# A two-layer transformer block on one core: weights times v in one row per attention unit, and the LayerNorm scale and shift between the layers applied when the rows are read back

## The chip, the cores and the metric

The kernel runs on one NeuronCore of a Trainium2 chip. The metric is device time in microseconds of one execution: 1528.76 us, the median of 3 runs (1528.45 to 1531.19). The engines are written as the profile writes them: PE (TensorE's products, PEld its weight loads), DVE (VectorE), ACT (ScalarE), POOL (GpSimd) and SP (SyncE, which issues the DMAs).

## The reference, cut to what matters

256 latent tokens and 256 context tokens of width 1024 go through two layers. In layer 1 only the latent tokens are carried on past the attention.

```python
for l in range(DEPTH):                       # DEPTH = 2
    o = token_mixer(x * (1 + sc1) + sh1, ...)   # A: windowed attention, B: global attention, C: RG-LRU,
                                                # three gated branches, one output projection
    x = layernorm(ALPHA * x + g1 * o, ln1_g[l], ln1_b[l])
    x = layernorm(ALPHA * x + g2 * mlp(x * (1 + sc2) + sh2), ln2_g[l], ln2_b[l])

def layernorm(x, g, b): return (x - mean) * rsqrt(var + eps) * g + b
def attend(q, k, v):    p = exp(s - m); return (p @ v) / sum(p)     # s = q @ k / 8, plus mask and sink in A
```

Everything is computed in float32. The attention has 8 query heads and 2 key heads in A and in B; one key head serves 4 query heads.

## The kernel before, in words

**Products.** A float32 operand is split into a high and a low part (`whi`, `wlo` for weights, `h_hi`, `h_lo` for rows), and each product is three passes: high by high, high by low, low by high. `mm` (L92) issues them, `tp` (L99) the transposes. The split is a cast (L120 on ACT or L122 on DVE) and a subtraction on DVE (L128). Projections with output channels on the partitions write a PSUM bank `ps_cm`, those with tokens on the partitions `ps_tm`. Weights arrive as units of 1 MB or less in the buffers `raw` (three of them, DMA at L186), are split piece by piece while the unit ahead of them is multiplied, and PE takes them in a fixed order.

**Attention.** The work of branches A and B is cut into units `(branch, key head, block of 128 tokens)`: 16 in layer 0 (8 of latent, 8 of context tokens) and 8 in layer 1. A unit has steps: its four heads of q transposed (`q_stage`, `ps_qT`); two score steps (`s_step`, `ps_s`, with the softmax on DVE and ACT after them); for each block of 128 keys (4 for a latent unit, 2 for a context unit) a transposing step (`t_step`: four transposes into `ps_pT`, then one copy on ACT into a tile `pT`); and a step of weights times v (`pv_step`: two products of 128 rows by 64 columns into the two halves of `ps_pv`). These two products are the ones that are not split in parts: they are plain float32, and PE shows two records for each. After a unit's last one the result is split into `y_hl`.

**The order of the work.** `attention` yields one step at a time, and `pair` interleaves it with projection work (the q projections of B, then the gates and branches of `MERGE[l]`). A step becomes due by a clock `self.pe` that adds a planned cost for each product: weights times v of one key block `lag_t` (3500 in layer 0, 2500 in layer 1) after that block's transposes, each transposing step at least `pace_t` (700) after the last one. So the key blocks of a unit are multiplied with v one at a time, with projection work, transposes or scores between them:

```python
if un["pv"] < un["t"]:
    opts.append((un["t_at"][un["pv"]] + lag_t, "pv"))
```

A scheduler then orders each engine's instructions under their dependencies; the buffers come from pools that rotate (63 tiles of 128x512 in the pool `gen`).

**LayerNorm between the layers.** After layer 0's MLP, `ln_z` (L1219, DVE) makes the normalised rows without scale and shift; the next layer's projections take scale and shift with their own modulation. The rows themselves are needed again 350 us later, as the residual of layer 1's output projection, with the scale and shift in them. `ln_x(0, 2)` does this at the start of layer 1, in the RG-LRU part (`lru`): it loads four tiles of scale and shift rows (`ln_rows`, L412), multiplies and adds on POOL (L1261, L1262, 8 instructions of 128x512), and writes the rows to DRAM (`xd`, L1263). `wout(1)` reads them back (L1334) at the start of the output projection. In that RG-LRU part PE needs the split weights of the first units, and DVE does the short convolution (L638), the splits of its result (`xc_hi`, `xc_lo`) and part of the weight splits.

Of the kernel before, what the change touches and what calls it, by code (L numbers as in the profile page):

```python
# [11 lines left out]
ALU = mybir.AluOpType  # L12
# [35 lines left out]
class Kern:  # L48
# [987 lines left out]
    def attention(self, l):  # L1036

        todo = deque((br, gr, tb) for br in "AB" for gr in range(2) for tb in ((2, 3, 0, 1) if l == 0 else (2, 3)))  # L1040
        left = {br: sum(u[0] == br for u in todo) for br in "AB"}
        live = []
        s_next = t_next = 0.0
        lag_q, lag_s, lag_t, pace_s, pace_t, depth_u = self.LAGS[l]
        while todo or live:
            now, soonest, step = self.pe, None, None
            for un in live:
                u, st = un["u"], un["st"]
                opts = []
                if un["pv"] < un["t"]:  # L1050
                    opts.append((un["t_at"][un["pv"]] + lag_t, "pv"))
                if un["s"] == 2 and un["t"] < un["n"]:
                    opts.append((max(un["s_at"] + lag_s, t_next), "t"))
                if un["s"] < 2:
                    opts.append((max(un["q_at"] + lag_q, s_next), "s"))
                for at, what in opts:
                    if at <= now:
                        step = (un, what)
                        break
                    soonest = at if soonest is None else min(soonest, at)  # L1060
                if step:
                    break
            if step is None and todo and len(live) < depth_u:
                u = todo[0]
                br, gr, tb = u
                ready = (l, "k", br) in self.flags and (l, "q") + u in self.flags
                if ready and now < self.qs_at[u] + (0, 4000)[l] and not self.idle_filler:
                    yield "wait"
                    continue
                if ready:  # L1070
                    if tb == 2:
                        self.k_stage(br, gr)
                        if gr == 0:
                            self.y[br] = [self.g2(l, "y_hl", F32R) for _ in range(4)]
                    todo.popleft()
                    self.q_stage(u)
                    live.append(dict(u=u, st=dict(p=[], pt={}, kt=self.kt), s=0, t=0, pv=0, n=4 if tb >= 2 else 2,
                                     t_at=[], q_at=self.pe))
                    yield
                    continue  # L1080
                if not live:
                    yield "need"
                    continue
            if step is None:
                if self.idle_filler:

                    self.pe = soonest
                else:
                    yield "wait"
                continue  # L1090
            un, what = step
            u, st = un["u"], un["st"]
            if what == "pv":
                last = un["pv"] == un["n"] - 1
                self.pv_step(u, un["pv"], st, last)
                un["pv"] += 1
                if last:
                    live.remove(un)
                    left[u[0]] -= 1
                    if left[u[0]] == 0:  # L1100
                        self.flags.add((l, "y", u[0]))
            elif what == "t":
                self.t_step(u, un["t"], st)
                un["t"] += 1
                un["t_at"].append(self.pe)
                t_next = self.pe + pace_t
            else:
                self.s_step(u, 2 * un["s"], st)
                un["s"] += 1
                un["s_at"] = self.pe  # L1110
                s_next = self.pe + (pace_s if u[2] >= 2 else pace_s / 2)
                if un["s"] == 2:
                    self.qt.pop(u)
            yield
# [134 lines left out]
    def ln_x(self, l, which):  # L1249


        nc = self.nc
        g, b = self.ln_rows(l, which)
        for tb in (range(4) if which == 1 and l == 0 else range(2, 4)):
            for hf in range(2):
                z = self.x[tb][hf]
                if which == 1:
                    for row, op in ((g[hf], ALU.mult), (b[hf], ALU.add)):
                        self.bg.append((2000, lambda z=z, row=row, op=op: nc.gpsimd.tensor_tensor(z, z, row, op=op), False))
                    continue  # L1260
                nc.gpsimd.tensor_tensor(z, z, g[hf], op=ALU.mult)  # L1261
                nc.gpsimd.tensor_tensor(z, z, b[hf], op=ALU.add)  # L1262
                nc.sync.dma_start(out=self.xd[128 * (tb - 2):128 * (tb - 1), 512 * hf:512 * hf + 512], in_=z)  # L1263

    def tail_units(self, l, which, keys, xs):

# [57 lines left out]

    def wout(self, l):
        self.start_residual(l, 1)
        self.x = {}
        for tb in self.tbs:
            r = slice(128 * (tb % 2), 128 * (tb % 2) + 128)
            src = (self.a["ctx"][0], self.a["x"][0])[tb // 2] if l == 0 else self.xd  # L1330
            self.x[tb] = []
            for hf in range(2):
                t = self.g("x")
                self.nc.sync.dma_start(out=t, in_=src[r, 512 * hf:512 * hf + 512])  # L1334
                self.x[tb].append(t)
        for h in range(2):
            self.unit((l, "wo", 0, h), self.take((l, "wo", 0, h)), self.m_hl(), self.tbs, True)
        self.tail_units(l, 1, [(l, "wo", 1, 0), (l, "wo", 1, 1)], self.m_hl())
        self.m = {}
# [110 lines left out]
    def layer(self, l):  # L1450
        a = self.a
        self.ada_start("layer%d" % l)
        self.layer_consts(l)
        self.ks, self.qs, self.qt, self.vv, self.y, self.m, self.tg, self.qs_at = {}, {}, {}, {}, {}, {}, {}, {}
        self.lru(l)
        if l == 0:
            self.run(self.kv(l, "A"))
            self.run(self.q(l, "A", 0))
            self.run(self.kv(l, "B"))

        def filler():
            if l == 0:
                yield from self.q(l, "A", 1)
            yield from self.q(l, "B", 0)
            yield from self.q(l, "B", 1)
            brs = [br for what, br in self.MERGE[l] if what == "br"]
            for what, br in self.MERGE[l]:
                self.ada_start(what + br + str(l))
                if what == "g":
                    yield from self.merge_gates(l, br)  # L1470
                else:
                    yield from self.merge_branch(l, br, br == brs[0], br == brs[-1])

        fl = filler()
        self.pair(self.attention(l), fl, (1.2, 2.0)[l])
        for _ in fl:
            pass
        self.h = None
        self.wout(l)
        self.ada_start("mlp%d" % l)  # L1480
        self.mlp(l)
# [95 lines left out]
```

## Time and profile before

| | |
|---|---|
| median of 3 runs | 1528.76 us |
| the profiled execution, its own time | 1529.95 us |
| span of that execution | 1528.2 us |
| PE busy | 1475.7 us, 97% |
| DVE busy | 1189.1 us, 78% |
| ACT busy | 743.7 us, 49% |
| POOL busy | 292.4 us, 19% |
| granted PE clock, mean | 0.985 |

One execution is profiled, and all durations below come from it; its own time is 1.75 us over its span. Columns of a timeline row are start (us from the span's start), duration (us), engine, line, operation, the tile written and those read, shapes, count, and in brackets how long the engine stood idle before it and what released it. Records of PE overlap, since the products are pipelined: what one costs is read from the distance of the starts. A row with `x4` stands for four records in a row. In rows by form, the number after `x` is the count, then busy us and the mean ns of one.

### The profile page before, as it was taken

What the parts mean: (1) busy time and instruction counts of PE and PEld (TensorE: products, weight loads), DVE (VectorE), ACT (ScalarE), POOL (GpSimd) and SP (SyncE); (2) the same over time, 40 slices, a digit from 0 to 9 for tenths busy, and PEclk for the clock granted to TensorE, in tenths of its full rate; (3) what the DMA queues carried; (4) which work ended last, traced back from release to release, by engine and by line L of the source; (5) the groups of instructions that cost most, each with busy time, mean ns of one, the idle gap of its engine ahead of it and who ended that gap; (6) DMA issues with size and microseconds to landing.
All of it is one profiled execution on the core that took longest, in us unless ns stands there. A gap on an engine that the chain in (4) does not pass through costs nothing.

```text
span 1528.2 us, 22367 instructions
## 1 busy us (share of the span) xinstructions
PE 1475.7 (97%) x8364; PEld 1226.4 (80%) x8364; DVE 1189.1 (78%) x2317; ACT 743.7 (49%) x1524; POOL 292.4 (19%) x302
## 2 busy tenths in 40 slices
PE   7799999999999999999999999899899999999997
PEld 4588988767778789778878887798777888899996
DVE  4689987848888968977657768979998665986667
ACT  2488766655323325413323232387766645555552
POOL 0523422100000002611110301545411000041110
PEclk9899999999999999999999999999999999999999
DMA  9522410013566653444535343243345633846663
GB/s 324 187 83 83 139 56 29 29 42 124 193 200 238 209 189 102 151 146 158 172 111 190 114 166 117 84 152 104 121 147 187 223 96 112 298 149 188 192 193 111
DMA packets 156748, 225.69 MB, mean 148 GB/s; under 512 B 5840, under 2 KB 118992, under 8 KB 151520
## 3 DMA queue, kind: packets, MB, share of 16 engines
q1 hardware_dynamic: 156640, 224.27, 44.6%
q8 instruction: 65, 1.06, 0.3%
q14 instruction: 43, 0.35, 0.1%
HBM read 218.97 MB, written 5.28 MB: 147 GB/s over the span
## 4 chain that ended last, share of the span: by engine, by line
PE 46%; DVE 9%; ACT 1%; issue 1%; POOL 0%; DVEq 0%
PE ps_cm L92 22%; PE ps_tm L92 19%; DVE wlo L128 2%; PE ps_pv L92 1%; PE ps_s L92 1%; PE ps_pT L99 1%; PE ps_gate L92 1%; DVE lru_q L709 1%; PE ps_ada L92 1%; DVE xc L638 1%; DVE lru_q L706 0%; DVE lru_i L699 0%; DVE xc_lo L128 0%; DVE rope L853 0%; DVE x L1219 0%
## 5 line engine op out<-in xcount | busy, mean ns | idle before, releaser
L120 ACT CAST whi<-raw 128x512 fp32r<-128x512 f32 x521 | 298.3, 619 | 404.6 <-PE ps_tm L92 199.7
L128 DVE TENSOR_TENSOR wlo<-raw,whi 128x512 fp32r<-128x512 f32 x560 | 404.1, 747 | 99.3 <-ACT whi L120 97.0
L92 PE MATMUL ps_cm<-h_hi,whi 128*128 128x256 f32 (+1 forms) x1216 | 413.5, 343 | 3.3 <-ACT whi L120 2.0
L92 PE MATMUL ps_cm<-h_hi,wlo 128*128 128x256 f32 (+1 forms) x1216 | 407.1, 336 | 6.3 <-DVE wlo L128 6.2
L92 PE MATMUL ps_cm<-h_lo,whi 128*128 128x256 f32 (+1 forms) x1216 | 407.5, 336 | 2.7 <-DVE h_lo L128 1.5
L92 PEld LDWEIGHTS ps_cm<-h_hi,whi 128*128 128x128 f32 x1216 | 231.6, 192 | 44.9 <-issue 14.8
L92 PEld LDWEIGHTS ps_cm<-h_hi,wlo 128*128 128x128 f32 x1216 | 231.8, 191 | 32.7 <-DVE wlo L128 9.1
L92 PEld LDWEIGHTS ps_cm<-h_lo,whi 128*128 128x128 f32 x1216 | 232.6, 192 | 26.6 <-DVE h_lo L128 2.8
L292 DVE SCALAR_TENSOR_TENSOR ada_acc<-raw_ada,silu,ada_acc 128x512 f32<-128x512 f32 x224 | 168.7, 801 | 49.8 <-DMA raw_ada<-in_w_ada_dram 49.6
L92 PE MATMUL ps_tm<-wlo,f_hi 128*128 128x512 f32 x384 | 150.6, 393 | 2.6 <-DVE wlo L128 2.6
L92 PE MATMUL ps_tm<-whi,f_hi 128*128 128x512 f32 x384 | 150.2, 392 | 0.0
L92 PE MATMUL ps_tm<-whi,f_lo 128*128 128x512 f32 x384 | 149.9, 391 | 0.0
L1181 POOL TENSOR_TENSOR x<-x,res 128x512 f32<-128x512 f32 x36 | 51.9, 1444 | 306.1 <-DVE res L1180 306.1
L92 PE MATMUL ps_tm<-wlo,h_hi 128*128 128x256 f32 x320 | 92.8, 290 | 7.5 <-DVE wlo L128 7.5
L92 PE MATMUL ps_tm<-whi,h_hi 128*128 128x256 f32 x320 | 94.2, 294 | 0.1
L92 PE MATMUL ps_tm<-whi,h_lo 128*128 128x256 f32 x320 | 91.9, 287 | 0.0
L92 PEld LDWEIGHTS ps_tm<-wlo,f_hi 128*128 128x128 f32 x384 | 72.5, 189 | 19.0 <-DVE wlo L128 4.1
L103 ACT ACTIVATE p<-ps_s,mx 128x512 f32<-128x512 f32 (+1 forms) x96 | 58.3, 614 | 56.8 <-DVE mx L993 29.9
L92 PEld LDWEIGHTS ps_tm<-whi,f_hi 128*128 128x128 f32 x384 | 72.5, 189 | 15.6 <-ACT whi L120 0.8
L92 PEld LDWEIGHTS ps_tm<-whi,f_lo 128*128 128x128 f32 x384 | 72.6, 189 | 15.0
L1241 POOL TENSOR_TENSOR h_lo<-hf,h_hi 128x256 fp32r<-128x256 f32 x28 | 23.2, 838 | 262.7 <-DVE h_hi L1240 260.7
L92 PEld LDWEIGHTS ps_tm<-wlo,h_hi 128*128 128x128 f32 x320 | 62.5, 195 | 9.6 <-DVE wlo L128 8.6
(172 smaller groups left out, 2489.4 us busy)
## 6 DMA issues: line engine op xcount, KB each, us to landing
raw<-in_w_ff_dram SPq DMA_DIRECT2D x64, 1024.0 KB, 5.2
raw<-in_w_in_dram SPq DMA_DIRECT2D x50, 1024.0 KB, 5.0
raw_ada<-in_w_ada_dram SPq DMA_DIRECT2D x40, 1024.0 KB, 5.0
w_ada<-in_w_ada_dram SPq DMA_DIRECT2D x32, 256.0 KB, 5.7
raw<-in_w_br_c_dram SPq DMA_DIRECT2D x8, 1024.0 KB, 5.1
raw<-in_w_out_dram SPq DMA_DIRECT2D x8, 1024.0 KB, 5.0
gw_raw<-in_v_gate_dram SPq DMA_DIRECT2D x16, 256.0 KB, 5.7
raw<-in_w_br_a_dram SPq DMA_DIRECT2D x8, 512.0 KB
```

The lines of the kernel that those rows point to most:

```text
L92: self.nc.tensor.matmul(out, lhsT, rhs, start=start, stop=stop, **kw)
L99: self.nc.tensor.transpose(out, in_, self.ident if n == 128 else self.ident[0:n, 0:n])
L103: ins = self.nc.scalar.activation(out, in_, func, **kw).ins
L120: self.nc.scalar.copy(out, in_)
L128: self.nc.vector.tensor_tensor(lo, src, hi.bitcast(F32), op=ALU.subtract)
L292: self.nc.vector.scalar_tensor_tensor(acc, w, c, acc, op0=ALU.mult, op1=ALU.add)
L638: nc.vector.scalar_tensor_tensor(o, r3[:, :, lo_ + d:lo_ + d + n], w(j), o, op0=ALU.mult, op1=ALU.add)
L709: nc.vector.tensor_tensor_scan(h[:, cs][:, ::-1], r[:, cs][:, ::-1], ig[:, cs][:, ::-1], init, op0=ALU.mult, op1=ALU.add)
L1181: (nc.vector if last else nc.gpsimd).tensor_tensor(x, x, t, op=ALU.add)
L1241: last = (nc.gpsimd if s == 0 or k % 2 else nc.vector).tensor_tensor(lo[:, c], h, hi[:, c].bitcast(F32), op=ALU.subtract)
```

## The change

Three things change.

1. In `attention`, a unit's weights times v become due only when all its key blocks have been transposed, `lag_t` after the last one, and then all its key blocks are issued one after the other in a single step. Before, each key block was a step of its own.
2. `ln_x` for the end of a layer (`which == 2`) writes the normalised rows to `xd` without scale and shift, loads no rows and uses no POOL.
3. The residual rows are read back in a new function `load_x`. In layer 0 it is called where the loop stood. In layer 1 it is called earlier, when the filler comes to branch B's gates in `MERGE[1]`, while the attention of B is under way; after each tile's load, POOL multiplies and adds there.

```diff
-                if un["pv"] < un["t"]:
-                    opts.append((un["t_at"][un["pv"]] + lag_t, "pv"))
-                if un["s"] == 2 and un["t"] < un["n"]:
+                if un["t"] == un["n"]:
+                    opts.append((un["t_at"] + lag_t, "pv"))
+                elif un["s"] == 2:
                     opts.append((max(un["s_at"] + lag_s, t_next), "t"))
...
             if what == "pv":
-                last = un["pv"] == un["n"] - 1
-                self.pv_step(u, un["pv"], st, last)
-                un["pv"] += 1
-                if last:
-                    live.remove(un)
...
+                for kc in range(un["n"]):
+                    self.pv_step(u, kc, st, kc == un["n"] - 1)
+                live.remove(un)
...
     def ln_x(self, l, which):
-        g, b = self.ln_rows(l, which)
+        if which == 1:
+            g, b = self.ln_rows(l, which)
...
-                nc.gpsimd.tensor_tensor(z, z, g[hf], op=ALU.mult)
-                nc.gpsimd.tensor_tensor(z, z, b[hf], op=ALU.add)
                 nc.sync.dma_start(out=self.xd[128 * (tb - 2):128 * (tb - 1), 512 * hf:512 * hf + 512], in_=z)
+
+    def load_x(self, l):
+
+        nc = self.nc
+        self.x = {}
+        if l:
+            g, b = self.ln_rows(l - 1, 2)
+        for tb in (range(4) if l == 0 else range(2, 4)):
+            r = slice(128 * (tb % 2), 128 * (tb % 2) + 128)
+            src = (self.a["ctx"][0], self.a["x"][0])[tb // 2] if l == 0 else self.xd
+            self.x[tb] = []
+            for hf in range(2):
+                t = self.g("x")
+                nc.sync.dma_start(out=t, in_=src[r, 512 * hf:512 * hf + 512])
+                if l:
+                    nc.gpsimd.tensor_tensor(t, t, g[hf], op=ALU.mult)
+                    nc.gpsimd.tensor_tensor(t, t, b[hf], op=ALU.add)
+                self.x[tb].append(t)
...
     def wout(self, l):
         self.start_residual(l, 1)
-        self.x = {}
-        for tb in self.tbs:
...
+        if l == 0:
+            self.load_x(l)
...
             for what, br in self.MERGE[l]:
                 self.ada_start(what + br + str(l))
+                if l and (what, br) == ("g", "b"):
+                    self.load_x(l)
```

How the instructions move, in the built programs. On PE, in layer 1 while branch C is merged (`ps_cm<-yc_hl` is that projection, `ps_pT` a transposing step, `ps_pv` weights times v; `x2` is one key block of a unit):

```order
 L92 MATMUL ps_cm<-yc_hl,whi 128x256 x2
 L92 MATMUL ps_cm<-yc_hl,wlo 128x256
-L99 MATMUL ps_pT<-ident,p 128x128 x4
-L92 MATMUL ps_cm<-yc_hl,whi 128x256 x2
-L92 MATMUL ps_cm<-yc_hl,wlo 128x256
-L92 MATMUL ps_cm<-yc_hl,whi 128x256 x2
-L92 MATMUL ps_cm<-yc_hl,wlo 128x256
-L92 MATMUL ps_pv<-pT,v 64x256 x2
+L92 MATMUL ps_pv<-pT,v 64x256 x8
 L92 MATMUL ps_cm<-yc_hl,whi 128x256 x2
 L92 MATMUL ps_cm<-yc_hl,wlo 128x256
```

The four key blocks of a unit now stand in one row of eight products. Over the whole program PE goes to weights times v 81 times before (49 in layer 0, 32 in layer 1) and 25 times now (16 and 9), with the same 160 products.

On POOL, at the start of layer 1 (`gw` are the split gate weights of the RG-LRU, `lru_i` its input gate):

```order
 L621 CAST gw_99<-gw_raw 128x512
 L622 TENSOR_TENSOR gw_100<-gw_raw,gw_99 128x512
 L621 CAST gw_101<-gw_raw 128x512
 L622 TENSOR_TENSOR gw_102<-gw_raw,gw_101 128x512
-L1261 TENSOR_TENSOR x<-x,ln_row 128x512 x3
-L1262 TENSOR_TENSOR x<-x,ln_row 128x512 x3
-L1261 TENSOR_TENSOR x<-x,ln_row 128x512
-L1262 TENSOR_TENSOR x<-x,ln_row 128x512
 L676 TENSOR_TENSOR lru_i<-lru_i,xc 128x512 x4
```

The eight instructions leave this place; they come back behind the last `gate_rows` of layer 1, with nothing else on POOL until the LayerNorm after the output projection. DVE's and ACT's rows are the same in both programs from layer 0's MLP to the start of layer 1's attention.

On SP's DMA queue, late in layer 1's attention (`raw<-in_w_in` are the four units of branch B's gate weights, `raw<-in_w_br_b` those of its projection):

```order
-L186 DMA raw<-in_w_in_dram 128x8x256 x4
+L186 DMA raw<-in_w_in_dram 128x8x256 x3
+L412 DMA ln_row<-in_ln_g_dram 128x512 x2
+L412 DMA ln_row<-in_ln_b_dram 128x512 x2
+L1275 DMA x<-xd 128x512 x4
+L186 DMA raw<-in_w_in_dram 128x8x256
 L186 DMA raw<-in_w_br_b_dram 128x4x256 x4
 L186 DMA raw<-in_w_out_dram 128x4x512 x4
 L412 DMA gate<-gd 128x512 x2
-L1334 DMA x<-xd 128x512 x4
```

Eight transfers now stand ahead of the fourth unit of gate weights, and four fewer ahead of the MLP's first weights. At the start of layer 1 the four row loads are gone from this queue, and the four writes to `xd` stand ahead of a weight load instead of behind two.

## Rows read from the trace of the kernel before

**Rows 1.** Busy time by stretch: layer 0's attention, the first part of layer 1's.

```profile
core 0: us, PE busy (x) PEld busy (x) DVE busy (x) ACT busy (x) POOL busy (x), PEclk, DMA share, GB/s
205.00:400.00 195.00, 194.81 (x1154) 145.79 (x1153) 147.15 (x399) 113.36 (x300) 24.09 (x46) 1.00 0.21 71
1138.00:1180.00 42.00, 40.35 (x300) 29.91 (x292) 36.52 (x94) 30.50 (x67) 4.56 (x8) 1.00 0.52 169
```

**Rows 2.** Timeline of PE, one key block of weights times v, layer 1.

```profile
1142.93 0.28 PE L92 MATMUL ps_cm<-h_lo,whi 128*128 128x256 f32 x1
1143.05 0.28 PE L92 MATMUL ps_cm<-h_hi,wlo 128*128 128x256 f32 x1
1143.26 0.65 PE L92 MATMUL ps_pv<-pT,v 128*64 128x256 f32 x4
1143.85 0.39 PE L92 MATMUL ps_cm<-h_hi,whi 128*128 128x256 f32 x1
1144.07 0.28 PE L92 MATMUL ps_cm<-h_lo,whi 128*128 128x256 f32 x1
```

**Rows 3.** The same in layer 0.

```profile
261.32 0.39 PE L92 MATMUL ps_cm<-h_hi,wlo 128*128 128x512 f32 x1
...
262.56 0.39 PE L92 MATMUL ps_cm<-h_lo,whi 128*128 128x512 f32 x1
262.79 0.39 PE L92 MATMUL ps_cm<-h_hi,wlo 128*128 128x512 f32 x1
```

**Rows 4.** Timeline of PE, sixteen plain float32 products in a row, program start.

```profile
19.08 3.65 PE L92 MATMUL ps_ada<-w_ada,silu 128*32 128x256 f32 x32
```

**Rows 5.** Instructions of the tile `ps_pv`: weight loads, min/median/max ns.

```profile
L92 PEld LDWEIGHTS ps_pv<-pT,v x320: 132/135/138, 211.4 to 1285.6; 128*64 128x64 f32 x160
```

**Rows 6.** Timeline of POOL, start of layer 1: first and last row of eight instructions.

```profile
975.77 4.10 POOL L1261 TENSOR_TENSOR x<-x,ln_row 128x512 f32<-128x512 f32 x3
...
985.73 1.33 POOL L1262 TENSOR_TENSOR x<-x,ln_row 128x512 f32<-128x512 f32 x1
```

**Rows 7.** DVE's instructions by form, 976.3 to 987.0, beside those on POOL.

```profile
L128 DVE TENSOR_TENSOR xc_lo<-xc,xc_hi 128x256 fp32r<-128x256 f32 x3 | 3.6, 1206 | 0.0
L128 DVE TENSOR_TENSOR wlo<-raw,whi 128x512 fp32r<-128x512 f32 x2 | 3.5, 1745 | 0.0
L122 DVE CAST whi<-raw 128x512 fp32r<-128x512 f32 x1 | 1.5, 1497 | 0.0
L122 DVE CAST xc_hi<-xc 128x256 fp32r<-128x256 f32 x2 | 1.5, 740 | 0.0
```

**Rows 8.** The same forms, 988.2 to 999.1, POOL idle almost throughout.

```profile
L128 DVE TENSOR_TENSOR wlo<-raw,whi 128x512 fp32r<-128x512 f32 x10 | 6.6, 684 | 0.2 <-ACT whi L120 0.2
L122 DVE CAST whi<-raw 128x512 fp32r<-128x512 f32 x5 | 2.1, 417 | 0.0
...
L128 DVE TENSOR_TENSOR xc_lo<-xc,xc_hi 128x256 fp32r<-128x256 f32 x2 | 0.8, 409 | 0.0
L122 DVE CAST xc_hi<-xc 128x256 fp32r<-128x256 f32 x2 | 0.6, 278 | 0.0
```

**Rows 9.** Timeline of PE in the same place: its waits.

```profile
984.58 0.58 PE L92 MATMUL ps_cm<-h_hi,wlo 128*128 128x256 f32 x1 [3.13 <-DVE wlo L128]
...
988.27 0.58 PE L92 MATMUL ps_cm<-h_hi,wlo 128*128 128x256 f32 x1 [1.48 <-DVE wlo L128]
```

**Rows 10.** Busy time and granted clock there.

```profile
985.00:990.00 5.00, 3.33 (x14) 2.74 (x14) 5.00 (x8) 0.00 (x0) 1.98 (x2) 0.50 0.00 0
```

**Rows 11.** Busy time by stretch, late in layer 1's attention.

```profile
1275.00:1290.00 15.00, 15.00 (x119) 12.86 (x118) 5.67 (x10) 8.55 (x18) 0.00 (x0) 1.00 0.22 72
```

**Rows 12.** Timeline of SP: loads of the third and fourth gate unit.

```profile
1261.71 0.37 SPq L186 DMA_DIRECT2D raw<-in_w_in_dram  x1
1266.56 0.37 SPq L186 DMA_DIRECT2D raw<-in_w_in_dram  x1
```

**Rows 13.** Waits of PE, whole program: line, releaser, us, times, longest.

```profile
PE ps_pv L92 <- ACT pT L120: 1.2, 1, 1.2
```

More of the change, by code (lines that the diff above doesn't have):

```diff
@@ L1076, in attention @@
                     self.q_stage(u)
-                    live.append(dict(u=u, st=dict(p=[], pt={}, kt=self.kt), s=0, t=0, pv=0, n=4 if tb >= 2 else 2,
-                                     t_at=[], q_at=self.pe))
+                    live.append(dict(u=u, st=dict(p=[], pt={}, kt=self.kt), s=0, t=0, n=4 if tb >= 2 else 2,
+                                     q_at=self.pe))
                     yield
@@ L1093, in attention @@
             if what == "pv":
-                last = un["pv"] == un["n"] - 1
-                self.pv_step(u, un["pv"], st, last)
-                un["pv"] += 1
-                if last:
-                    live.remove(un)
-                    left[u[0]] -= 1
-                    if left[u[0]] == 0:
-                        self.flags.add((l, "y", u[0]))
+                for kc in range(un["n"]):
+                    self.pv_step(u, kc, st, kc == un["n"] - 1)
+                live.remove(un)
+                left[u[0]] -= 1
+                if left[u[0]] == 0:
+                    self.flags.add((l, "y", u[0]))
             elif what == "t":
@@ L1104, in attention @@
                 un["t"] += 1
-                un["t_at"].append(self.pe)
+                un["t_at"] = self.pe
                 t_next = self.pe + pace_t
@@ L1326, in wout @@
         self.start_residual(l, 1)
-        self.x = {}
-        for tb in self.tbs:
[L1329 to L1335, printed above, removed]
+        if l == 0:
+            self.load_x(l)
         for h in range(2):
```

## The prediction

> **What bounds the kernel now.** I read the page's table of engines first: PE is busy for 97% of the span, so a gain has to come out of what PE does, or out of the 3% in which it stands. Busy time by stretch says where. In layer 0's attention PE is busy for 194.81 of 195 us while DVE has 147.15 and ACT 113.36; in the first part of layer 1's it has 40.35 of 42, but DVE 36.52 and ACT 30.50, so that there a shorter PE soon meets the splits [rows 1]. "Busy" hides what a change of product costs, so the next view is PE's timeline around one key block of weights times v, in layer 1 [rows 2] and layer 0 [rows 3], and beside it the only place where such plain float32 products stand sixteen in a row [rows 4]. For the second part I read POOL's timeline at the start of layer 1 [rows 6], DVE's instructions by form beside it and just behind it [rows 7, 8], PE's waits in the same place [rows 9] and its clock [rows 10]. For the third, the stretch where the work goes [rows 11] and the queue it enters [rows 12].
>
> **Weights times v in a row.** Nothing is added or removed: 160 products, which PE goes to 25 times and not 81. What changes is the price of going there. In layer 1 the `ps_cm` product ahead of a key block starts at 1143.05 and the second one behind it at 1144.07: 1.02 us, in which two `ps_cm` products also ran. Such a product takes one step of 0.12 between starts (1142.93 to 1143.05), so the key block, two products with two records each, cost 1.02 - 0.24 = 0.78 [rows 2]. In layer 0, with products of 512 columns, again with one `ps_cm` product in between: 1.24 less two steps of 0.23 is 0.78 too [rows 3]. The records themselves say 0.65 for the four, so the page's busy time would not show this.
>
> What a product costs when its neighbours are of its own kind is the row of sixteen: 3.65 us for 32 records, 0.23 a product, with the run-out of the last one in it [rows 4]. A key block inside a row then costs 0.46 and not 0.78, and each visit that is folded into another saves 0.32. 81 - 25 = 56 visits go: **17.9 us**. I take two things off. By a count along PE's rows some 22 of the old visits stood beside another of attention's short products, where part of the 0.32 is paid for the neighbour anyway: 1.0, an estimate (at most 22 x 0.32 = 7.0). And of the 23 visits that go in layer 1, I put a third, 8 x 0.32 = 2.5 us, in the stretch where DVE has 36.52 of 42 us and the time may not come out at the end: half of it, 1.2. That leaves **15.7**.
>
> What the row adds is a later first product: it waits for the unit's last key block, and ACT's copy of it into `pT`. PE's order keeps the planned distance between transposes and row full of projection products, and in the kernel before PE waited for such a copy once, 1.2 us [rows 13]. Normally I cost this at nothing, with those products as cover; without the cover it is a rival below. The unit's result is read by a projection whole units later.
>
> **POOL's work leaves the start of layer 1.** Eight instructions run there from 975.77 to 987.06 [rows 6], 11.3 us. POOL isn't on PE's path, but DVE is. Beside POOL, DVE's subtraction `wlo` takes 1745 ns and behind it 684; `xc_lo` 1206 and 409; the casts 1497 and 417, 740 and 278 [rows 7, 8]. In counts of rows 7: 2 x 1.06 + 3 x 0.80 + 1 x 1.08 + 2 x 0.46 = 2.1 + 2.4 + 1.1 + 0.9 = 6.5 us of DVE's time. PE waits for just these splits, 3.13 and 1.48 us [rows 9], and after the first wait runs at a granted clock of 0.50, the 1.2 GHz level, through 985 to 990, where its 3.33 busy us would take half at full clock, 1.7 [rows 10]. Seen from PE that is 3.13 + 1.48 + 1.7 = 6.3, from DVE 6.5. I take **6.3**: DVE is busy throughout here and its order is the same in both programs, so what it sheds comes off PE's waits. Bounds: 3.1 (the second wait and the clock stay, because DVE is still the slower one and the PE rests briefly for the next split) and 6.5. Four row loads also leave SP's queue here, and the writes to `xd` pass ahead of a weight load; the waits in this place are for DVE [rows 9], so nothing.
>
> **The same work, late.** POOL gets its 11.3 us back near 1270 to 1285. DVE is busy there for 5.67 of 15 us and PE all of it [rows 11]: DVE has room to be slow. Were every DVE instruction there stretched as in rows 7, the most would be the old 6.5 and a clock drop of 1.7. SP issues eight transfers ahead of the fourth gate unit, 8 x 0.37 = 3.0 us of queue by the issues of rows 12. That unit's load followed the third's by 4.85 us [rows 12], waiting for its buffer, and so the eight fit in the gap if their own tiles are free; if not, the load and its splits come late by some 2 us. At the start of the output projection four read-backs no longer stand ahead of the MLP's first weights; those are needed a whole projection later, so nothing. Between 0 and -8.2, I take **-1.0**, near the end with cover because DVE has 9 of 15 us free.
>
> **Sum.** 15.7 + 6.3 - 1.0 = 21.0 us. The profiled execution took 1529.95 us (its span 1528.2 and 1.75 around it); 1508.95 is its counterpart, and since it lies 1.2 over the median of the runs, the forecast is **1508 us**.
>
> **The rivals.**
> *The loads of a row show.* Each record has a weight load of its own, 135 ns at the median [rows 5]. If PE can't hide those of neighbours in a row, a product there costs 0.135 more and a folded visit saves 0.32 - 0.27 = 0.05: 56 x 0.05 = 2.8 in place of 15.7 (less its deductions), and the sum is 8.1, **1520.6 us**. Against it: the sixteen in a row had such loads too and took 0.23 apiece with them in [rows 4]; and PEld is busy for 145.79 of 195 us beside a PE that hardly stands, also with 128 rows in use [rows 1]. For it: the loads of rows 4 were of 32 columns, these are of 64. 9%. The Trainium skill ("TensorE: Matmul & The Clock Gate", Part 3, The mechanism) says that a weight load overlaps running products only where its row group differs, and both kinds here use all 128 rows; by that rule the time would come out as this rival's. The rows of this case lean the other way.
>
> *The late work locks DVE when it is wanted.* The attention's last units and the splits of branch B's gates are due there too. If POOL's eight instructions meet the two-operand subtractions as before, the price is that of the start, 6.5 + 1.7 = 8.2 in place of 1.0: 13.8, **1515 us**. For it: these subtractions are still being done there. Against: PE stood nowhere in that stretch, with DVE idle for most of it [rows 11]. 12%. The Trainium skill ("SBUF — State Buffer", Who interferes with whom) says that a DVE instruction with two SBUF inputs and a POOL instruction that reads SBUF exclude each other for their whole length. The trace agrees (684 to 1745 ns), and by that rule moving the work moves the lock with it; what it costs is then only a question of who waits.
>
> *The start of layer 1 doesn't give.* Another wait may end last there, such as ACT's half of the weight splits: 15.7 - 1.0 = 14.7, **1514 us**. For it: PE stands or crawls from 980 to 990 with several feeders at work; against: the waits all name DVE [rows 9]. 12%.
>
> *Slower: rows that wait.* If ACT, which copies each `pT`, is behind its plan by more than the planned distance at the end of each unit, every one of the 25 rows waits as PE did once, 1.2 us [rows 13]: 25 x 1.2 = 30 against a gain of 21, **1538 us**. It decides from 21 / 25 = 0.84 us of wait a row on. Before, a late copy held up one key block; now it holds the row. Against it: one such wait among 81 visits, with ACT at 58% in layer 0 [rows 1]. 5%.
>
> That the change doesn't do what it says is excluded by the order of the built program: the rows of eight, and POOL's move, stand there.
>
> **How the numbers follow.** Forecast 62%; the rivals 9, 12, 12 and 5%. Within the forecast no deduction and 6.5 at the start give 17.9 + 6.5 = 24.4, 1504.3, and the three runs differ by 2.7 us, so the low end is 1502. The high end takes in the second and third rival and two small ones together (1515 with half the start lost is 1518) and stops at 1520, just under the first rival. What this kernel's runs can tell from no change is about 0.2%, 3 us. Only the fourth rival is slower: 5%. No change needs the first and the second together (8.1 - 7.2 = 0.9, 1528): 2%. The rest, 93%, is faster.
>
> **What would show it.** Right: PE's rows of `ps_pv` take 0.22 to 0.24 us a product from start to start, some 3.7 for a row of sixteen records; no wait of 3.13 before 985 and a granted clock near 1.00 from 985 to 990; `wlo` near 684 ns there; from then on layer 1 early by some 15 us. POOL's eight instructions near the end of attention, with DVE's `wlo` beside them long and PE without a wait. Wrong: rows at 0.36 a product (first rival); waits of PE on `wlo` or on the fourth gate unit's load late in attention (second); a new wait at 980 to 990 with another name (third); a list of waits where `ps_pv` on `pT` has gone from 1.2 us to tens (fourth).

## The result, and the profile after

1512.26 us (1510.67 to 1512.75, 4 runs) against 1528.61 for the kernel before on the same chip: ratio 0.9892, interval 0.9873 to 0.9911, which is 13.6 to 19.4 us faster. The profiled execution has a span of 1510.3 us, against 1528.2. The forecast was 1508 (20.8 us faster) and the range 1502 to 1520.

Where the time went is read by laying the two traces side by side: the start of the same PE product (the 107th `ps_tm<-whi,h_hi`, at 199 us before, and so on) in both, and the distances between such marks. I chose seven marks: the program up to q's transposes in layer 0 (0 to 199 us before), layer 0's attention and branches (to 525), the rest of layer 0 (to 973), the start of layer 1 (to 1015), its RG-LRU and keys (to 1121), and its attention in two halves (to 1246, to 1317).

| us, change less before | 0-199 | 199-525 | 525-973 | 973-1015 | 1015-1121 | 1121-1246 | 1246-1317 | sum |
|---|---|---|---|---|---|---|---|---|
| the change | -0.9 | -2.6 | -0.1 | -7.6 | +1.3 | -5.7 | -2.4 | -18.0 |

The first stage has the same instructions in the same order in both programs; among the executions shown below it lies between -4.2 and +0.5 of the one of before. That much is an execution's own, and so the stages, not the sums, are compared below.

**Weights times v.** PE's timeline of the change, layer 1, one row:

```profile
1158.32 0.28 PE L92 MATMUL ps_cm<-h_hi,wlo 128*128 128x256 f32 x1
1158.53 1.95 PE L92 MATMUL ps_pv<-pT,v 128*64 128x256 f32 x16
1160.41 0.39 PE L92 MATMUL ps_cm<-h_hi,whi 128*128 128x256 f32 x1
1160.63 0.28 PE L92 MATMUL ps_cm<-h_lo,whi 128*128 128x256 f32 x1
```

From 1158.32 to 1160.63 are 2.31 us with two `ps_cm` steps of 0.12: the row of four key blocks costs 2.07 where four visits cost 4 x 0.78 = 3.12 [rows 2]. Each of the three visits that went saved 0.35, a little over the 0.32 of the forecast. The 23 that went in layer 1 are worth 23 x 0.35 = 8.05; the last two stages of the table give 5.7 + 2.4 = 8.1. PE's waits hardly enter this: in these two stages they are 2.5 us before and 2.2 now. One for DVE's `wlo`, 1.22 us at 1147.75, is new, and those for `pT`, 1.2, and for `p`, 0.5, are gone.

**The start of layer 1.** Busy time by stretch and, below it, DVE's forms from 970 to 986, the same place:

```profile
980.00:985.00 5.00, 5.00 (x37) 4.69 (x36) 5.00 (x14) 2.51 (x6) 0.00 (x0) 1.00 0.63 210
985.00:990.00 5.00, 5.00 (x29) 4.25 (x28) 4.72 (x7) 4.99 (x8) 2.59 (x2) 1.00 0.51 172
```

```profile
L128 DVE TENSOR_TENSOR wlo<-raw,whi 128x512 fp32r<-128x512 f32 x9 | 5.9, 680 | 0.0
...
L128 DVE TENSOR_TENSOR xc_lo<-xc,xc_hi 128x256 fp32r<-128x256 f32 x6 | 2.5, 417 | 0.0
```

PE doesn't stand any more, the clock that was granted is full where it had been 0.50 [rows 10], and `wlo` takes 680 ns and not 1745 [rows 7].

**Layer 0** is where the forecast's gain is missing. Busy time, and PE's waits over the whole program:

```profile
205.00:400.00 195.00, 190.40 (x1169) 154.07 (x1168) 143.47 (x394) 113.59 (x301) 22.85 (x46) 0.99 0.22 73
```

```profile
PE ps_s L92 <- ACT qT L120: 3.5, 3, 2.3
...
PE ps_pT L99 <- DVE p L1008: 0.8, 2, 0.6
```

PE stood for 0.19 us in this stretch before [rows 1]; now for 4.6. The longest wait is new, at 223.28, and it is for the copy of q's transposes. PE's timeline, then ACT's:

```profile
217.33 0.60 PE L99 MATMUL ps_qT<-ident,qstk 128*128 128x128 f32 x4
...
223.28 0.74 PE L92 MATMUL ps_s<-kT,qT 128*128 128x256 f32 x4 [2.34 <-ACT qT L120]
...
224.82 0.41 PE L92 MATMUL ps_tm<-whi,h_hi 128*128 128x256 f32 x1
```

```profile
220.24 0.48 ACT L103 ACTIVATE p<-ps_s,mx 128x256 f32<-128x256 f32 x1 [1.27 <-PE ps_pT L99]
...
221.98 0.27 ACT L120 CAST y_hl<-ps_pv 128x128 fp32r<-128x128 f32 x1 [0.36 <-DVE y_hl L128]
222.14 0.59 ACT L120 COPY pT<-ps_pT 128x512 f32<-128x512 f32 x1
222.62 0.60 ACT L120 CAST qT<-ps_qT 128x512 fp32r<-128x512 f32 x1
```

The transposes were done by 218, but ACT takes its instructions in order, and between stood an older unit's softmax, which itself waited for 1.27 us, two casts of a finished row and a copy of `pT`. PE meanwhile ran out of what stood ahead of the scores in its own order: 6 us lie between the transposes and the scores here, waiting included, and 8.0 lay between them before, filled with visits to weights times v and what stood between those. PE of the kernel before:

```profile
219.95 0.60 PE L99 MATMUL ps_qT<-ident,qstk 128*128 128x128 f32 x4
...
221.98 0.65 PE L92 MATMUL ps_pv<-pT,v 128*64 128x256 f32 x4
...
224.27 0.65 PE L92 MATMUL ps_pv<-pT,v 128*64 128x256 f32 x4
...
225.88 0.65 PE L92 MATMUL ps_pv<-pT,v 128*64 128x256 f32 x4
...
227.96 0.64 PE L92 MATMUL ps_s<-kT,qT 128*128 128x256 f32 x4
```

Behind the wait its clock was at the lower level for some microseconds:

```profile
223.00:229.00 6.00, 5.72 (x36) 5.73 (x37) 4.28 (x17) 3.94 (x13) 1.70 (x4) 0.72 0.01 3
```

(1 - 0.72) x 6 = 1.7 us. (Two kernels below with the same order in layer 0 have the same waits but kept a clock of 0.99 and 1.00 there; their stage is -4.4 and -4.1.) The third loss is neither: the sums of the modulation (`ps_ada<-ada_acc`), a row of sixteen records before, stand later in PE's order and in three pieces. PE of the kernel before, then of the change:

```profile
439.06 0.39 PE L92 MATMUL ps_cm<-y_hl,wlo 128*128 128x512 f32 x1
439.37 1.92 PE L92 MATMUL ps_ada<-ada_acc,pick 128*32 128x512 f32 x16
441.23 0.74 PE L92 MATMUL ps_cm<-y_hl,whi 128*128 128x512 f32 x2
```

```profile
444.98 0.39 PE L92 MATMUL ps_cm<-y_hl,wlo 128*128 128x512 f32 x1
445.30 1.06 PE L92 MATMUL ps_ada<-ada_acc,pick 128*32 128x512 f32 x6
446.29 0.50 PE L92 MATMUL ps_cm<-h_hi,whi 128*128 128x512 f32 x1
...
447.32 0.39 PE L92 MATMUL ps_cm<-h_lo,whi 128*128 128x512 f32 x1
447.64 1.06 PE L92 MATMUL ps_ada<-ada_acc,pick 128*32 128x512 f32 x8
448.63 0.51 PE L92 MATMUL ps_cm<-h_hi,wlo 128*128 128x512 f32 x1
449.07 1.05 PE L92 MATMUL ps_ada<-ada_acc,pick 128*32 128x512 f32 x2
450.05 0.50 PE L92 MATMUL ps_cm<-h_hi,whi 128*128 128x512 f32 x1
```

Before, 441.23 - 439.06 less a step of 0.23 is 1.94 us. Now the three visits take 1.31 + 1.31 + 1.42 less three steps, 3.35: 1.4 us more for the same products. The three pieces stand in all nine traces with rows in layer 0, and the one row in all five without. Together: 33 visits at 0.32 are 10.6; less 4.4 of new waits, 1.7 of clock and 1.4 leaves 3.1, where the table has 2.6.

### The profile page after: what moved, and what is told of

Its sections match the earlier page's. It is cut to its first block, busy times and chain, and to the rows that moved or that the text cites. A ratio compares the mean times of both kernels' runs of the same rounds, so it can differ in the third digit from the quotient of the medians.

```text
span 1510.3 us, 22369 instructions
## 1 busy us (share of the span) xinstructions
PE 1458.7 (97%) x8364; PEld 1230.3 (81%) x8364; DVE 1182.7 (78%) x2317; ACT 744.4 (49%) x1524; POOL 292.6 (19%) x302
## 4 chain that ended last, share of the span: by engine, by line
PE 82%; DVE 12%; ACT 3%; issue 1%; DMA 1%; SPq 0%; POOL 0%; DVEq 0%; ACTq 0%
PE ps_cm L92 44%; PE ps_tm L92 26%; DVE wlo L128 3%; PE ps_s L92 2%; PE ps_pv L92 2%; PE ps_ada L92 2%; PE ps_pT L99 2%; PE ps_gate L92 2%; DVE lru_q L709 1%; PE ps_qT L99 1%; DVE xc L638 1%; DVE ada_acc L292 1%; DVE lru_i L699 1%; DVE lru_q L706 1%; ACT L103 1%
## 5 line engine op out<-in xcount | busy, mean ns | idle before, releaser
L676 POOL TENSOR_TENSOR lru_i<-lru_i,xc 128x512 f32<-128x512 f32 x32 | 53.6, 1698 | 95.5 <-ACT lru_i L103 95.5
```

Of the source, the lines that this page charges most:

```text
L676: nc.gpsimd.tensor_tensor(ig, ig, self.xc[k[0]][0], op=ALU.mult)
```

## The experiments

Ratios are to the kernel before, five rounds each. The stages are those of the table above; only the four that tell something are shown.

| kernel | median us | ratio | 199-525 | 973-1015 | 1121-1246 | 1246-1317 |
|---|---|---|---|---|---|---|
| rows alone | 1518.78 | 0.9935 (0.9919 to 0.9950) | -4.4 | +0.4 | -5.7 | -2.4 |
| LayerNorm's moves alone | 1527.46 | 0.9989 (0.9978 to 1.0000) | 0.0 | -7.6 | 0.0 | +4.2 |
| rows in layer 1 alone | 1515.45 | 0.9906 (0.9889 to 0.9922) | 0.0 | -7.6 | -5.7 | -2.4 |
| change, distance 3200 | 1506.54 | 0.9861 (0.9843 to 0.9880) | -6.6 | -7.6 | -5.7 | -2.4 |
| LayerNorm's moves, late work left out | 1521.22 | 0.9938 (0.9922 to 0.9955) | 0.0 | -7.6 | 0.0 | +0.4 |
| change, late work left out | 1512.38 | 0.9881 (0.9865 to 0.9896) | -4.1 | -7.6 | -5.7 | -2.4 |
| rows of two, 3200 | 1522.02 | 0.9946 (0.9932 to 0.9959) | -3.7 | -7.6 | -0.6 | +3.3 |
| rows in layer 1 alone, 3200 | 1516.32 | 0.9903 (0.9886 to 0.9919) | -0.2 | -7.6 | -5.7 | -2.4 |
| the change again | 1510.97 | 0.9877 (0.9860 to 0.9895) | -2.7 | -7.6 | -5.7 | -2.4 |
| change, 3200, again | 1507.72 | 0.9863 (0.9848 to 0.9879) | -6.2 | -7.6 | -5.7 | -2.4 |
| change, distance 4800 | 1505.25 | 0.9846 (0.9830 to 0.9863) | -6.7 | -7.6 | -5.7 | -2.4 |
| rows of two, 3200, late work left out | 1517.94 | 0.9934 (0.9914 to 0.9954) | -2.7 | -7.6 | -1.0 | -1.1 |

**Each part alone.** Rows alone: the kernel before with `attention` of the change.

> The kernel before with the rows of weights times v alone; LayerNorm's scale and shift stay at the start of layer 1. Theory A (each place in the program gives what the two traces show when they are laid side by side): layer 0's rows 2.6 us, layer 1's 6.9, so 9.5 us under before, and layer 0 shows PE waiting some 4 us for ACT's qT and DVE's p. Theory B (the forecast's price of a visit holds and something else is slower in the change): 15 to 18 us under before. Theory C (the rows are worth little, the gain is LayerNorm's): under 4 us.

Measured 9.9 us (7.6 to 12.4) under before: theory A. The same waits for `qT` (2.25 and 0.73) and `p` stand in layer 0 of its trace.

LayerNorm's moves alone: the change with `attention` of before.

> The kernel before with LayerNorm's two moves alone; weights times v stay one key block at a time. Theory A: 7.6 us under before, PE's waits of 3.13 and 1.48 at 980 to 990 gone and the clock there full; POOL's eight instructions late in layer 1's attention cost PE less than 1 us. Theory B (the late work locks DVE and takes part back, which the rows hide in the change): 0 to 4 us under before, with new waits of PE between 1262 and 1290.

Measured 1.7 us (0 to 3.4): theory B. The start of layer 1 gives its 7.6, and the last stage takes 4.2 back. The parts don't add: 9.9 + 1.7 is 11.6, and the change has 16.5. PE's timeline in that last stage, then DVE's and the busy time:

```profile
1272.62 0.44 PE L99 MATMUL ps_pT<-ident,p 128*128 128x128 f32 x2 [1.39 <-DVE p L1008]
...
1274.02 0.44 PE L99 MATMUL ps_pT<-ident,p 128*128 128x128 f32 x2 [0.85 <-DVE p L1008]
```

```profile
1268.16 2.99 DVE L128 TENSOR_TENSOR wlo<-raw,whi 128x512 fp32r<-128x512 f32 x3 [2.94 <-ACT whi L120]
...
1271.26 2.70 DVE L1008 TENSOR_SCALAR p<-p,den 128x512 f32<-128x512 f32 x2
```

```profile
1265.00:1280.00 15.00, 12.76 (x89) 10.69 (x88) 7.68 (x8) 6.58 (x15) 10.91 (x8) 0.89 0.53 173
```

POOL is busy for 10.91 of these 15 us, and DVE's scaling of `p` by its sum, two instructions, takes 2.70 us. Waits of 2.2 and (1 - 0.89) x 15 = 1.7 of clock are nearly the whole 4.2.

**Was it POOL's work or the eight transfers?** In the kernel of LayerNorm's moves, and in the change, the multiplications and additions at the late place are left out; the transfers stay.

```diff
-                if l:
-                    nc.gpsimd.tensor_tensor(t, t, g[hf], op=ALU.mult)
-                    nc.gpsimd.tensor_tensor(t, t, b[hf], op=ALU.add)
```

> The kernel of LayerNorm's moves alone, but the eight multiplications and additions late in layer 1's attention are left out (the residual rows go on without scale and shift); the eight transfers stay, and PE's order is the same. Theory A (POOL's late work locks DVE where it scales p, as it did at the start of layer 1): PE's waits of 1.39 and 0.85 for p at 1272 to 1275 go and the clock stays full: 4 us faster than LayerNorm's moves alone, 5 to 8 under before. Theory B (the eight transfers ahead of branch B's projection weights, or ACT's order, make p late): the waits stay, the time is within 1 us of LayerNorm's moves alone.

> The change with the same eight instructions left out late in layer 1's attention (the residual rows go on without scale and shift). Theory A (with the rows, the last unit's p is already scaled when POOL starts, so the lock only slows weight splits that nobody waits for): within 1.5 us of the change. Theory B (the late work costs the change as much as it costs LayerNorm's moves alone): some 4 us faster than the change.

Theory A both times. With LayerNorm's moves alone the last stage goes from +4.2 to +0.4, and DVE's timeline there reads:

```profile
1269.17 0.88 DVE L1008 TENSOR_SCALAR p<-p,den 128x512 f32<-128x512 f32 x2
1270.03 0.69 DVE L128 TENSOR_TENSOR wlo<-raw,whi 128x512 fp32r<-128x512 f32 x1
```

0.88 in place of 2.70. (Its 9.5 us under before are more than the stages show; 4.2 of its profiled execution's 8.7 are in the first stage, where nothing differs.) In the change nothing differs: 0.9881 and 0.9892, and the same -2.4. There DVE was already through with `p` when POOL began. DVE and, below, POOL in the change:

```profile
1251.62 0.88 DVE L1008 TENSOR_SCALAR p<-p,den 128x512 f32<-128x512 f32 x2
...
1254.73 4.67 DVE L128 TENSOR_TENSOR wlo<-raw,whi 128x512 fp32r<-128x512 f32 x4
...
1261.39 4.79 DVE L128 TENSOR_TENSOR wlo<-raw,whi 128x512 fp32r<-128x512 f32 x3 [0.29 <-ACT whi L120]
```

```profile
1255.75 1.41 POOL L1277 TENSOR_TENSOR x<-x,ln_row 128x512 f32<-128x512 f32 x1 [52.97 <-PE ps_pT L99]
```

The lock is there, with `wlo` at 1.6 us at the median and up to 1.8; but PE doesn't wait at all in this stage. With rows the last unit's softmax stands earlier in the order, 3.3 us ahead of POOL. It is a near thing, as the rows of two show below.

**Layer 0's rows.** First without them, in layer 0 alone:

```diff
-                if un["t"] == un["n"]:
-                    opts.append((un["t_at"] + lag_t, "pv"))
-                elif un["s"] == 2:
+                if l == 0 and un["pv"] < un["t"]:
+                    opts.append((un["t_at"][un["pv"]] + lag_t, "pv"))
+                if l == 1 and un["t"] == un["n"]:
+                    opts.append((un["t_at"][-1] + lag_t, "pv"))
+                if un["s"] == 2 and un["t"] < un["n"]:
...
```

> The change with its rows in layer 1 alone; layer 0 goes to each key block by itself, as before. Theory A (layer 0's rows earn little, since the waits for qT and p take their gain back): 2 to 4 us slower than the change, 13 to 15.5 under before. Theory B (layer 0's rows earn their 33 x 0.32 = 10.6 and the clock or some other part of layer 0 is slower for another reason): some 10 us slower than the change, 6 to 8 under before.

The ratio is 0.0014 above the change's, 2.1 us, and the stage loses the 2.6: theory A. Then with them and one number altered, the planned distance in layer 0 from a unit's q transposes to its scores:

```diff
-    LAGS = ((1600, 5500, 3500, 3000, 700, 3), ...
+    LAGS = ((3200, 5500, 3500, 3000, 700, 3), ...
```

> The change with one number altered: the planned distance in layer 0 from a unit's q transposes to its scores goes from 1600 to 3200. Theory A (PE waits in layer 0 because rows leave fewer products between these transposes and the scores, while ACT's copy of qT stands behind older units' work): the waits of 2.34 and 0.74 for qT go, the low clock after them too, 3 to 5 us faster than the change. Theory B (ACT and DVE are behind in layer 0 as a whole): the waits move to p and pT, and the time stays within 1 us of the change.

> The change with the longer distance in layer 0 (3200) once more, on the same chip as the change. Theory A (the waits for qT and the low clock behind them are what it saves): 3 to 6 us faster than the change. Theory B (the earlier difference was the chip's or the program start's): within 1.5 us.

Theory A: 5.7 us under the change's first median, 3.3 beside the change on one chip. The intervals of those last two overlap, so this rests on the stage: -6.2 and -6.6 where the change's order has -2.6 to -4.4. PE's waits from 205 to 400 in the first of the two, and busy time:

```profile
PE ps_qT L99 <- DVE qstk L897: 0.9, 1, 0.9
PE ps_pT L99 <- DVE p L1008: 0.4, 1, 0.4
PE ps_pv L92 <- ACT p L103: 0.3, 1, 0.3
```

```profile
205.00:400.00 195.00, 193.03 (x1187) 156.35 (x1186) 146.64 (x405) 114.45 (x307) 26.59 (x46) 1.00 0.22 74
```

The waits for `qT` are under 0.2 us or gone, PE has 193.0 us of 195 and the clock is full. What PE still stands is for other tiles, and the modulation's sums are in three pieces here too: 31 visits went, 31 x 0.32 = 9.9, less 1.8 of new waits and 1.4, leaves 6.7. The control is the same number without rows in layer 0:

> Rows in layer 1 alone, with the longer distance in layer 0 (3200): the control for that number. Theory A (without rows in layer 0 PE doesn't wait for qT, so the number is worth nothing there): within 1.5 us of rows in layer 1 alone, 12 to 15 under before, and some 7 slower than the change with that distance. Theory B (the number helps whatever the rows do): 4 to 6 us faster than rows in layer 1 alone.

Theory A: 0.9903 and 0.9906. Only beside the rows is the number worth something. More of it:

> The change with the distance in layer 0 from q's transposes to the scores at 4800. Theory A (once the copy of qT is in time, more distance is worth nothing): within 1.5 us of 3200. Theory B (the distance still eats waits for p and pT): 1.5 to 3 us faster than 3200.

The median is 2.5 us lower, which speaks for theory B, but the intervals overlap and the stage is within 0.5 of 3200's, while the first stage, with nothing changed in it, differs by 1.6. I leave it at "no slower". The repeat of the change, for the comparison on one chip:

> The change itself once more, beside the next three on one chip. 15 to 19 us under before; the waits of PE for qT in layer 0 (2.34 and 0.74) are there again if they belong to its order and not to one execution.

18.9 us under before; the waits for `qT` are there again, 2.33 and 0.73.

**The price of a visit.** Two key blocks in a step, 49 visits of PE in place of 27:

```diff
-                if un["t"] == un["n"]:
-                    opts.append((un["t_at"] + lag_t, "pv"))
-                elif un["s"] == 2:
+                if un["t"] >= un["pv"] + 2:
+                    opts.append((un["t_at"][un["pv"] + 1] + lag_t, "pv"))
+                if un["s"] == 2 and un["t"] < un["n"]:
...
-                for kc in range(un["n"]):
+                for kc in (un["pv"], un["pv"] + 1):
```

> The change with the longer distance in layer 0 (3200), and rows of two key blocks in place of four: 49 visits of PE to weights times v and not 27. Theory A (a visit costs 0.32 to 0.35 us more than going on in the row): 22 visits more, 7 us slower than the change with that distance, some 15 under before. Theory B (most of the price was paid by something else, such as a later release): within 2 us of it.

13 us slower than rows of four by the ratios, not 7, so neither theory's number. The last stage, +3.3, looks like that of LayerNorm's moves alone, and the trace has `p` in it again, two waits of PE (2.6 and 0.4) for an instruction of up to 1491 ns. So, once more without the late work:

> Rows of two key blocks with the longer distance in layer 0, and the eight instructions late in layer 1's attention left out (the residual rows go on without scale and shift); PE's order is that of rows of two. Theory A (of the 12 us that rows of two lost, 5 to 6 were the lock that met p again, since they put the last unit's p back beside POOL's work; the rest is 22 visits at 0.32 to 0.35): 5 to 6 us faster than rows of two, 6 to 8 slower than rows of four with that distance. Theory B (a visit costs 0.55 and the late work nothing): as slow as rows of two.

The last stage goes from +3.3 to -1.1, 4.4 us of lock, with `p` at 487 ns at most. The medians don't show it: the ratios are 0.0012 apart, within their intervals, where theory A had 5 to 6 us, and the kernel is 10.2 us slower than rows of four with that distance on the same chip, where it had 6 to 8. So this rests on the stage and on the instruction. In layer 1's attention 14 visits more than with rows of four now cost 8.1 - 2.1 = 6.0, 0.43 each, with 0.5 us more of waits in it (2.7 in all against 2.2); without these 0.39. In layer 0 there are 8 visits more, and its stage is 3.5 to 3.9 us behind. By the stages it is theory A's mechanism, with 4.4 us of lock and a visit at some 0.4; its two numbers for the whole were not met.

## Why the prediction was right, and where it was off

The range held the time, and the two parts that were to gain gained; the time came out 4.3 us above the forecast. That it wasn't more is partly luck: layer 0 fell short by 7 to 8 us, and three other terms were too small, by 1.9 (layer 1's visits), 1.3 (start of layer 1) and 1.0 (the late place). Step by step, by the stages:

- *Price of a visit:* 0.32 forecast, 0.35 in the rows, and 8.1 us in layer 1 in each kernel that has these rows. The 1.2 taken off for DVE's share there wasn't needed: the wait for `wlo` that it stood for came, 1.22 us, but old waits of 1.7 went. The sign "some 3.7 for a row of sixteen records" was misread from [rows 4], where 3.65 us are 32 records; sixteen are eight products, 1.8 at that price, and the row shown above lasts 1.95.
- *Layer 0:* this is the step that failed: "Normally I cost this at nothing, with those products as cover". 10.6 us were in the sum (33 x 0.32, before the 1.0); 2.6 came, or 4.4 at best where the clock held. I had allowed for a wait at the row itself, for `pT`, and the change's rows have none. It came elsewhere: fewer pieces of PE work between a unit's q transposes and its scores, and ACT's queue full of older units' work at that place. Altering that one distance brought some 2 to 4 of it back, and did nothing where there are no rows. The split of the modulation's sums comes with the rows in every trace, but wasn't tried by itself; why they are split is not shown.
- *Start of layer 1:* 6.3 forecast, 7.6 measured in all the kernels with the move. The waits named were the right ones; behind them the clock of the kernel before had been low beyond 990 too, 0.88 from 990 to 995, another (1 - 0.88) x 5 = 0.6 that I hadn't counted:

```profile
990.00:995.00 5.00, 5.00 (x37) 4.91 (x37) 5.00 (x13) 0.82 (x2) 0.00 (x0) 0.88 0.67 178
```

- *The late place:* -1.0 forecast, 0 measured, but only since the rows had moved the last softmax ahead of POOL. Without them it costs 4.2. The rival had the lock, but at twice that price (8.2), and with the weight splits as what PE waits for, where it was the scaling of `p`.
- *Weight loads of a row show* (first rival): no. In a row its records start 7 and 209 ns apart in turn, 0.216 us a product, where the rival had 0.36. Each record has a load of 137 ns at the median; the two of a product start 7 ns apart as well, and their records lie beside those of the product ahead; nothing of their time shows in the step. The Trainium skill's sentence ("TensorE: Matmul & The Clock Gate", Part 3, The mechanism), that loads overlap only with products of another row group, is not what these rows of 128-row products show.
- *Slower:* no row waited for `pT` in the change.

The stage from 1015 to 1121, where PE waits some 9 us, 7.5 of them for DVE's `wlo`, gave +1.3 in the change and between -1.9 and +2.9 in the others, with the same order too. What sets it in one execution is left open.

## What to carry to other kernels

Price a change of product by the distance between starts on either side of a visit, and then look for what the many small visits were covering for: not the step you merge, but the next in-order hand-over through another engine. Work that locks DVE is not made free by moving it to where DVE is idle on average; what counts is whether an instruction somebody waits for stands beside it, and another part of the same change can decide that. And measure the parts together as well as apart: here they were 4.9 us better together by the medians, and 4.2 by the last stage.

## What the runs showed of the hardware

The scaling of `p`, one tensor input and a scalar for each partition, was held up beside POOL's work as much as the two-input subtractions: 482 ns and 1486. The Trainium skill ("SBUF — State Buffer", Who interferes with whom) lists this operation among those that can take the shared port pair; the trace agrees, and the row is 1004 ns longer.

The price of three stages repeated to 0.1 us from execution to execution (-7.63 or -7.64 in twelve traces with the move, -5.7 and -2.4 in nine with rows of four in layer 1), while the first 199 us, which nothing touched, differed by up to 4.7. Layer 0's attention did not repeat so well, -2.6 to -4.4 in four traces with one order, nor did the stage from 1015 to 1121. For a change of a few microseconds in a stage that repeats, two traces side by side told more than the medians.
